# Emitting and pinning one tile's turn behind the last tile's mean and squares

## The chip, the cores and the metric

The kernel runs on one core of one Trainium2 chip. The metric is the device time of one execution in microseconds (us). Engine names are those of the profile: PE is the matmul engine, PEld its weight loads, DVE the vector engine, ACT the scalar engine, POOL the general-purpose engine, SP the engine that issues the transfers here.

## What is computed

Two trunk layers of a diffusion backbone run over 128 context tokens and 512 latent tokens, model width 1024, with shared weights. Each layer has two sublayers, a mixer and a gated convolutional FFN, and each sublayer ends in the same way:

```python
hp = xp * (1 + sc1c) + sh1c                      # modulated input of the mixer
xp = _layernorm(ALPHA * xp + g1c * dp, ln1_g[l], ln1_b[l])
hp = xp * (1 + sc2c) + sh2c                      # modulated input of the FFN
fp = _conv_ffn(hp, ...)
xp = _layernorm(ALPHA * xp + g2c * fp, ln2_g[l], ln2_b[l])
```

The same is done for the latent tokens (`xs`). All arithmetic is in float32; matrix products are made from three products of a high and a low part.

## The kernel before

**Tiles.** The 640 tokens are five tiles of 128 tokens, numbered 0 to 4 (tile 0 is the context). At a sublayer's end `project` goes over the five tiles: for tile i it makes two products of 128x512 (both halves of the width) on PE, `accumulate` multiplies them by a gate and adds them to the residual `ys[i]` on DVE (L498, L502; the L502 instruction also sums the row), and `Norm.stats(i)` makes the layer norm.

**Stats.** `stats(i)` emits, in this order: the negated mean on DVE (L367) and the same over 32 (L368); the sum of squares on ACT (L370, "the squares" below); `affine(i - 1)`, the scale and shift of the tile before with the next sublayer's modulation folded in (L417 multiply, L420 add, for two halves; for tile 3 all four run on DVE and the multiplies are pinned); for tile 4 alone a quicker form on DVE (L377 twice, later L399 twice in `second`); `rstd_of` on POOL (L161, L162); then `between()`; then the normalisation of `ys[i]` in place (L385 on POOL, L389 on ACT). For i of 2 and up `between` is `turn(i - 2)`.

**Turn.** `turn(i)` brings tile i's modulated rows into columns for the next sublayer: for each half of the width four PE transposes into one PSUM tile `B` (L434), then four `split`s, two on each half. A split is a cast on ACT to the high part (L99, reads PSUM) and a subtraction on DVE to the low part (L102, reads the same PSUM tile and the high part). After the loop `project` starts the next sublayer: `next(nxt)` emits its first product over tokens 0 to 257 (24 matmuls of 258 columns, L155 to L157), then `turn(3)`, then a second such product of 24, then `turn(4)`. Tokens 258 to 641, which are tiles 2, 3 and 4, come in a second group of products of 384 columns each, called the second token group below.

**Order.** SP's queue runs as emitted. For the other engines a scheduler orders each queue ahead of the run, by its own estimate of durations and of what is ready, earlier emitted work first. `keep_in_program_order` pins one instruction behind the instruction that was emitted just before it on its engine. Buffers come from pools that are handed on in turn; `ht` and the squares' scratch are of the six `t` buffers.

**Ends.** There are four sublayer ends. At three of them (near 212, 700 and 1043 us) a next sublayer follows; at the last there is no turn.

Of the kernel before, what the change touches and what calls it, by code (L numbers as in the profile page):

```python
# [41 lines left out]
def tile_hybrid_trunk(ctx, tc, xT, x, vecs, tabs, wm0, wm1, wmT, crow, grow, lnrow, bs, w_u, w_v, w_p, w_s, w_pool, w_eo,  # L42
# [4 lines left out]
    dve, act, pe, pool, sp = nc.vector, nc.scalar, nc.tensor, nc.gpsimd, nc.sync  # L47
# [28 lines left out]
    def Tm(shape, dt=F32):  # L76
        return tpool.tile(shape, dt, tag="t", name=nm("t"))

    def M(shape, dt=F32):
        return mpool.tile(shape, dt, tag="m", name=nm("m"))  # L80
# [10 lines left out]
    def B():  # L91
        return psB.tile([128, 512], F32, tag="B", name=nm("B"))

    def f(ap):
        return ap.bitcast(F32)

    def split(hi, lo, src, hi_eng, lo_eng):
        if hi_eng is act:
            act.copy(hi, src)  # L99
        else:  # L100
            hi_eng.tensor_copy(hi, src)
        return lo_eng.tensor_tensor(lo, src, f(hi), ALU.subtract)  # L102


# [16 lines left out]
    def prep(lo_eng=None, pin=False):  # L121
        if not loaded:
            load()
        raw, shape, scale, lo_ = loaded.pop(0)
        lo_eng = lo_eng or lo_
        hi, lo = W(shape, F32R), W(shape, F32R)
        if scale is not None:
            act.activation(hi, raw, AF.Identity, scale=scale)
            dve.scalar_tensor_tensor(lo, raw, scale, f(hi), ALU.mult, ALU.subtract)
            ready.append((hi, lo))  # L130
            return
        with tc.high_priority() if urgent[0] else ExitStack():
            i = split(hi, lo, raw, act, lo_eng or pool)
        if pin:
            tc.keep_in_program_order(i)
        ready.append((hi, lo))
# [22 lines left out]
    def rstd_of(v, e):  # L159
        r = M([128, 1])  # L160
        pool.tensor_tensor(v, v, eps[:, e:e + 1], ALU.add)  # L161
        pool.tensor_tensor(r, v, eps[:, 2:3], ALU.pow)  # L162
        return r
# [168 lines left out]
    def pad_h(h):  # L332
        for t in h[0] + h[1]:
            pool.memset(f(t[:, :, 128:130]), 0.0)
# [16 lines left out]
    class Norm:  # L351
# [11 lines left out]
        def stats(self, i, sums, between=None):  # L363
            y = ys[i]
            a, b = self.rows(i)
            nm, sm, v, nb = (M([128, 1]) for _ in range(4))
            dve.tensor_scalar(nm, sums[0], sums[1], -1.0 / 1024.0, ALU.add, ALU.mult)  # L367
            dve.tensor_scalar(sm, nm, 1.0 / 32.0, None, ALU.mult)  # L368
            jk = Tm([128, D], mybir.dt.bfloat16)
            act.activation(jk, y, AF.Square, bias=sm, scale=1.0 / 32.0, accum_out=v)  # L370
            if i and not self.fast(i - 1):
                self.affine(i - 1)
            if self.fast(i):
                self.ht[i] = [Tm([128, 512]), Tm([128, 512])]
                for h in range(2):
                    sl = slice(h * 512, h * 512 + 512)
                    dve.scalar_tensor_tensor(self.ht[i][h], y[:, sl], nm, a[:, sl], ALU.add, ALU.mult)  # L377
            r = self.rs[i] = rstd_of(v, 0)
            if between is not None:
                between()  # L380
            if i == 4:
                self.second(4)
            if self.nxt is None and self.fast(i):
                return
            pool.tensor_tensor(nb, nm, r, ALU.mult)  # L385
            n = 1 if i == 4 else 2
            for h in range(n):
                sl = slice(h * D // n, (h + 1) * D // n)
                act.activation(y[:, sl], y[:, sl], AF.Identity, bias=nb, scale=r)  # L389
# [35 lines left out]
        def turn(self, i):  # L425
            hi, lo = self.h
            if i == 0:
                pad_h(self.h)
            c = slice(TOK[i], TOK[i] + 128)
            p4 = []  # L430
            for half in range(2):
                ps = B()
                for k in range(4):
                    pe.transpose(ps[:, k * 128:(k + 1) * 128], self.ht[i][half][:, k * 128:(k + 1) * 128], ident)  # L434
                p4.append(ps.rearrange("p (k t) -> p k t", k=4))
            for s in range(4):
                split(hi[s][:, :, c], lo[s][:, :, c], p4[s // 2][:, 2 * (s % 2):2 * (s % 2) + 2, :], act, dve)

        def lazy(self, n=1, out=None):
            w = D // n  # L440
# [93 lines left out]
    def ffn(l, h):  # L534
# [33 lines left out]
        def finish(p, tg, tv):  # L568
            dve.tensor_tensor(tv, tv, tg, ALU.mult)  # L569
            q = max(q for q in range(NQ) if PIECES[q] <= p)  # L570
            gh, gl = pieces[q]
            n = p - PIECES[q]
            if n % 2 == 0:
                gh.append(S([128, 2, T], F32R))
                gl.append(S([128, 2, T], F32R))
            split(gh[n // 2][:, n % 2, :], gl[n // 2][:, n % 2, :], tv, act, dve)
# [99 lines left out]
    def even_first(cb):  # L676
# [90 lines left out]
        with tc.manual_schedule(engines={mybir.EngineType.PE}):  # L767
            warm(16)
            r = mod(0)
            warm(3)  # L770
            turn(0, r)
            for e in (dve, pool, dve):
                prep(e)
            us.extend([take(), take()])
            vu.append(take())
            warm(8)
            r = mod(1)
            for e in range(8):
                product(e, 0)
                if e < 7:  # L780
                    turn(e + 1, r)
                product(e, 1)
                product(e, 2)
                if e < 6:
                    r = mod(e + 2)
                    if e + 5 < 8:
                        load_w(e + 5)
                        load_x(e + 5)
                        if e == 1:
                            load()  # L790
                product(e, 3)
                if e in (0, 2, 4):
                    prep()
                    vu.append(take())
# [762 lines left out]
```

## Time and profile before

| | us |
|---|---|
| median of 3 runs | 1525.19 (1523.65 to 1526.64) |
| profiled execution, its own time | 1525.87 |
| its span, first to last instruction | 1524.1 |
| around the span | 1.8 |

In the rows below, a line of the timeline gives the start in us, the duration in us, the engine, the line of the code, the operation, output<-inputs, shapes, and in brackets how long the engine sat idle before it and what ended that. The mean granted TensorE clock of the whole span is 0.985 of full speed.

### The profile page before, as it was taken

Reading aid. Unit: us, or ns where it says so; the run is one execution under the profiler, and the core shown is the slowest. Engines: PE = TensorE matmul, PEld = TensorE weight load, DVE = VectorE, ACT = ScalarE, POOL = GpSimd, SP = SyncE. Lnnn points to the kernel's source line nnn. Section 1 sums busy time; section 2 is a strip of 40 time slices with the busy share of each in tenths; the row PEclk is TensorE's granted clock in tenths of the full one; section 3 lists DMA queues with packets and bytes.
Section 4 is the critical chain, followed back from the end, with each engine's and each line's share of the span. In section 5 each row is a group of like instructions: output and inputs, shape, how many; then the busy total and the mean of one; then the engine's idle time right before and its main releaser. Section 6 shows DMA issues by size and latency. Waiting matters only on the chain. (4 is left out here: it accounts for less than half of the span.)

```text
span 1524.1 us, 21977 instructions
## 1 busy us (share of the span) xinstructions
PE 1458.7 (96%) x8768; PEld 1316.2 (86%) x8768; DVE 987.7 (65%) x1500; ACT 597.7 (39%) x889; POOL 541.8 (36%) x434
## 2 busy tenths in 40 slices
PE   7989999999999999999997999998999999999997
PEld 5866879989898989888987888787999989898995
DVE  4685688456878697768698477768763334333557
ACT  3422354333132323235775566536333313232223
POOL 2241444333242424543453101864313231232343
PEclk9999999999999999999999999999999999999999
DMA  9544705344454555341321003342433322133231
GB/s 375 219 157 166 277 12 199 107 140 161 157 167 139 164 164 170 99 140 52 112 74 46 1 2 125 122 156 87 162 111 124 99 70 83 34 116 101 71 110 69
DMA packets 54757, 188.10 MB, mean 123 GB/s; under 512 B 6592, under 2 KB 7168, under 8 KB 54656
## 3 DMA queue, kind: packets, MB, share of 16 engines
q1 hardware_dynamic: 54656, 186.71, 36.3%
q8 instruction: 69, 1.13, 0.3%
q14 instruction: 32, 0.26, 0.1%
HBM read 175.96 MB, written 10.72 MB: 122 GB/s over the span
## 5 line engine op out<-in xcount | busy, mean ns | idle before, releaser
L102 POOL TENSOR_TENSOR w<-r,w 128x1024 fp32r<-128x1024 f32 (+2 forms) x133 | 334.6, 2526 | 682.9 <-ACT w L99 667.2
L155 PE MATMUL A<-s,w 128*128 128x258 f32 (+1 forms) x1672 | 524.7, 314 | 19.7 <-ACT t L1227 8.0
L156 PE MATMUL A<-s,w 128*128 128x258 f32 (+1 forms) x1672 | 522.6, 313 | 0.5 <-DVE s L102 0.5
L157 PE MATMUL A<-s,w 128*128 128x258 f32 (+1 forms) x1672 | 521.8, 312 | 0.0
L155 PEld LDWEIGHTS A<-s,w 128*128 128x128 f32 x1672 | 318.0, 190 | 30.8 <-issue 14.7
L156 PEld LDWEIGHTS A<-s,w 128*128 128x128 f32 x1672 | 318.8, 191 | 4.3 <-issue 2.5
L157 PEld LDWEIGHTS A<-s,w 128*128 128x128 f32 x1672 | 318.6, 191 | 2.5 <-issue 2.5
L99 ACT CAST w<-r 128x1024 fp32r<-128x1024 f32 (+2 forms) x181 | 183.8, 1033 | 342.3 <-PE B L156 136.3
L155 PE MATMUL B<-w,s 128*128 128x512 f32 (+2 forms) x734 | 282.9, 387 | 3.5 <-DVE y L495 2.1
L156 PE MATMUL B<-w,s 128*128 128x512 f32 (+2 forms) x734 | 282.4, 385 | 2.3 <-DVE w L102 2.3
L157 PE MATMUL B<-w,s 128*128 128x512 f32 (+2 forms) x734 | 281.4, 384 | 1.0 <-DVE s L102 1.0
L558 DVE SCALAR_TENSOR_TENSOR t<-A,vec,t 128x641 f32<-128x641 f32 x88 | 77.7, 883 | 210.8 <-ACT t L557 210.6
L155 PEld LDWEIGHTS B<-w,s 128*128 128x128 f32 x734 | 138.3, 189 | 32.0 <-DVE y L495 2.3
L156 PEld LDWEIGHTS B<-w,s 128*128 128x128 f32 x734 | 138.4, 189 | 30.1 <-DVE w L102 3.3
L157 PEld LDWEIGHTS B<-w,s 128*128 128x128 f32 x734 | 138.4, 189 | 29.1 <-DVE s L102 1.4
L250 DVE SCALAR_TENSOR_TENSOR t<-r,v 128x1024 bf16<-128x1024 f32 x112 | 160.1, 1440 | 4.7 <-DMA r<-in_wmT_dram 3.7
L99 ACT CAST s<-t 128x642 fp32r<-128x642 f32 x60 | 43.8, 730 | 183.0 <-DVE t L569 147.8
L102 DVE TENSOR_TENSOR w<-r,w 128x1024 fp32r<-128x1024 f32 (+3 forms) x48 | 69.6, 1466 | 61.5 <-ACT w L99 61.4
L495 DVE TENSOR_TENSOR y<-B,y 128x512 f32<-128x512 f32 x80 | 54.7, 687 | 62.3 <-PE B L157 62.2
L557 ACT ACTIVATE t<-A,vec 128x642 f32<-128x642 f32 x88 | 77.6, 882 | 13.9 <-PE A L157 13.8
L559 DVE SCALAR_TENSOR_TENSOR t<-A,vec,t 128x641 f32<-128x641 f32 x88 | 77.8, 885 | 2.5
L561 ACT ACTIVATE t<-t 128x642 f32<-128x642 f32 x44 | 32.6, 742 | 101.6 <-DVE t L559 95.8
(260 smaller groups left out, 1602.7 us busy)
## 6 DMA issues: line engine op xcount, KB each, us to landing
r<-in_w_up_dram SPq DMA_DIRECT2D x88, 512.0 KB, 3.7
r<-in_wmT_dram SPq DMA_DIRECT2D x56, 512.0 KB, 3.3
r<-in_w_dn_dram SPq DMA_DIRECT2D x44, 512.0 KB, 4.2
s<-scr SPq DMA_DIRECT2D x20, 512.0 KB, 7.5
s<-in_wm_dram SPq DMA_DIRECT2D x16, 512.0 KB, 9.3
r<-in_wm_dram SPq DMA_DIRECT2D x16, 512.0 KB, 4.6
kept<-y SPq DMA_DIRECT2D x10, 512.0 KB, 3.5
r<-kept SPq DMA_DIRECT2D x10, 512.0 KB, 3.5
```

The costliest lines, as they stand in the source:

```text
L99: act.copy(hi, src)
L102: return lo_eng.tensor_tensor(lo, src, f(hi), ALU.subtract)
L155: pe.matmul(out, ah, bh, start=i == 0, stop=False)
L156: pe.matmul(out, ah, bl, start=False, stop=False)
L157: pe.matmul(out, al, bh, start=False, stop=i == n - 1)
L250: op = dve.scalar_tensor_tensor(junk, raw, 1.0, cb[s], ALU.mult, ALU.mult, accum_out=mc[l][:, m, s, k:k + 1])
L495: dve.tensor_tensor(acc[i][:, sl], ps, acc[i][:, sl], ALU.add)
L557: act.activation(t, z, AF.Identity, bias=cb, scale=w1)
L558: dve.scalar_tensor_tensor(t[:, 1:], z[:, :T - 1], w0, t[:, 1:], ALU.mult, ALU.add)
L559: dve.scalar_tensor_tensor(t[:, :T - 1], z[:, 1:], w2, t[:, :T - 1], ALU.mult, ALU.add)
L561: act.activation(t, t, AF.Silu)
```

## The change

At tile 4 `between()`, which there is `turn(2)`, is called right after the squares instead of after `rstd_of`. The turn of tile 2 is pinned: each of its ACT casts stands behind the ACT instruction emitted before it (for the first cast that is tile 4's squares), each of its DVE subtractions behind the DVE instruction emitted before it (for the first that is L368 of tile 4), for tile 2 alone. Since `affine(3)` is now emitted after the turn and its L417 was pinned already, L417 of tile 3 now stands behind the turn's last subtraction. No instruction, buffer or transfer is added or removed. At the last sublayer end `between` is None and nothing changes.

```diff
--- before.py
+++ after.py
@@ -94,11 +94,13 @@
     def f(ap):
         return ap.bitcast(F32)
 
-    def split(hi, lo, src, hi_eng, lo_eng):
+    def split(hi, lo, src, hi_eng, lo_eng, pin_hi=False):
         if hi_eng is act:
-            act.copy(hi, src)
+            op = act.copy(hi, src)
         else:
-            hi_eng.tensor_copy(hi, src)
+            op = hi_eng.tensor_copy(hi, src)
+        if pin_hi:
+            tc.keep_in_program_order(op)
         return lo_eng.tensor_tensor(lo, src, f(hi), ALU.subtract)
 
 
@@ -368,6 +370,9 @@
             dve.tensor_scalar(sm, nm, 1.0 / 32.0, None, ALU.mult)
             jk = Tm([128, D], mybir.dt.bfloat16)
             act.activation(jk, y, AF.Square, bias=sm, scale=1.0 / 32.0, accum_out=v)
+            if i == 4 and between is not None:
+                between()
+                between = None
             if i and not self.fast(i - 1):
                 self.affine(i - 1)
             if self.fast(i):
@@ -434,7 +439,9 @@
                     pe.transpose(ps[:, k * 128:(k + 1) * 128], self.ht[i][half][:, k * 128:(k + 1) * 128], ident)
                 p4.append(ps.rearrange("p (k t) -> p k t", k=4))
             for s in range(4):
-                split(hi[s][:, :, c], lo[s][:, :, c], p4[s // 2][:, 2 * (s % 2):2 * (s % 2) + 2, :], act, dve)
+                op = split(hi[s][:, :, c], lo[s][:, :, c], p4[s // 2][:, 2 * (s % 2):2 * (s % 2) + 2, :], act, dve, i == 2)
+                if i == 2:
+                    tc.keep_in_program_order(op)
 
         def lazy(self, n=1, out=None):
             w = D // n
```

## Rows read from the trace of the kernel before

**Rows 1.** The page, part 1: an engine's busy us, share of the span, instructions.

```profile
PE 1458.7 (96%) x8768; PEld 1316.2 (86%) x8768; DVE 987.7 (65%) x1500; ACT 597.7 (39%) x889; POOL 541.8 (36%) x434
```

**Rows 2.** Line L434: what ended PE's idle time before a transpose (us, times).

```profile
  DVE t L420: 15.0, 6
```

**Rows 3.** Timeline of PE at the first of the three ends.

```profile
209.86 0.36 PE L155 MATMUL A<-s,w 128*128 128x258 f32 x1
...
213.44 0.29 PE L157 MATMUL A<-s,w 128*128 128x258 f32 x1
216.12 0.88 PE L434 MATMUL B<-ident,t 128*128 128x128 f32 x4 [2.40 <-DVE t L420]
...
219.17 0.92 PE L434 MATMUL B<-ident,t 128*128 128x128 f32 x4
...
220.77 1.04 PE L434 MATMUL B<-ident,t 128*128 128x128 f32 x8
221.96 0.62 PE L155 MATMUL A<-s,w 128*128 128x384 f32 x2 [0.15 <-ACT s L99]
```

**Rows 4.** Timeline of PE at the second and the third end.

```profile
703.88 0.66 PE L434 MATMUL B<-ident,t 128*128 128x128 f32 x4 [2.40 <-DVE t L420]
...
709.59 0.61 PE L155 MATMUL A<-s,w 128*128 128x384 f32 x2
...
1046.99 0.66 PE L434 MATMUL B<-ident,t 128*128 128x128 f32 x4 [2.38 <-DVE t L420]
...
1051.37 0.62 PE L155 MATMUL A<-s,w 128*128 128x384 f32 x2
```

**Rows 5.** Timeline of ACT at the first end.

```profile
211.44 1.52 ACT L389 ACTIVATE y<-y,m,m 128x512 f32<-128x512 f32 x2 [2.41 <-POOL m L385]
212.87 0.62 ACT L99 CAST s<-B 128x256 fp32r<-128x256 f32 x2
213.71 0.82 ACT L99 CAST s<-B 128x256 fp32r<-128x256 f32 x2 [0.22 <-DVE s L102]
214.43 1.15 ACT L370 ACTIVATE t<-y,m 128x1024 bf16<-128x1024 f32 x1
```

**Rows 6.** Timeline of DVE at the first end.

```profile
211.28 0.08 DVE L502 DVE_READ_ACCUMULATOR y<-t,y 128x1 f32 x1
213.25 0.42 DVE L102 TENSOR_TENSOR s<-B,s 128x256 fp32r<-128x256 f32 x1 [1.89 <-ACT s L99]
213.59 0.20 DVE L367 TENSOR_SCALAR m<-m,m 128x1 f32<-128x1 f32 x1
...
214.45 0.68 DVE L417 TENSOR_TENSOR t<-y,s 128x512 f32<-128x512 f32 x1
...
215.38 0.68 DVE L420 TENSOR_TENSOR t<-t,s 128x512 f32<-128x512 f32 x1
...
216.59 0.75 DVE L377 SCALAR_TENSOR_TENSOR t<-y,m,s 128x512 f32<-128x512 f32 x1
...
218.51 1.41 DVE L399 SCALAR_TENSOR_TENSOR t<-t,m,s 128x512 f32<-128x512 f32 x2
```

**Rows 7.** Timeline of POOL at the first end.

```profile
216.19 0.89 POOL L162 TENSOR_TENSOR m<-m,eps 128x1 f32<-128x1 f32 x1
```

**Rows 8.** Timeline of ACT at the second and the third end.

```profile
699.20 1.52 ACT L389 ACTIVATE y<-y,m,m 128x512 f32<-128x512 f32 x2 [2.40 <-POOL m L385]
...
1042.30 1.52 ACT L389 ACTIVATE y<-y,m,m 128x512 f32<-128x512 f32 x2 [2.40 <-POOL m L385]
```

**Rows 9.** Stretches: PE, PEld, DVE, ACT, POOL busy (instructions), granted clock, DMA share, GB/s.

```profile
95.80:100.20 4.40, 4.39 (x20) 4.40 (x21) 3.60 (x6) 1.46 (x2) 0.00 (x0) 0.50 0.38 119
...
216.40:219.80 3.40, 3.40 (x18) 3.40 (x17) 3.40 (x6) 0.38 (x1) 0.90 (x2) 0.50 0.00 0
817.40:820.50 3.10, 3.08 (x14) 3.08 (x15) 2.88 (x3) 1.66 (x3) 1.63 (x4) 0.50 0.00 0
...
1046.90:1051.30 4.40, 4.28 (x34) 3.87 (x34) 4.40 (x9) 2.13 (x5) 1.18 (x3) 1.00 0.00 0
```

## The prediction

> **What bounds the kernel now.** I read the page first: PE is busy for 96% of the span [rows 1], so what this change can move is PE's idle time, and its clock, at three sublayer ends. Next I asked for the transposes at L434. Their largest wait is for DVE's L420, the end of `affine(3)`: 15.0 us over six waits, 7.2 of them the one long wait that each end shows [rows 2, 3, 4]. Then came the timelines of PE, ACT and DVE at the first end. PE issues 30 matmuls (24 of the next sublayer's first product, six of the second) from 209.86 to 213.44, sits idle for 2.40 us, does tile 3's first transposes at 216.12, and from there to 221.96, where the second token group starts, it works without a gap: 16 transposes and the 18 matmuls that were left [rows 3]. DVE is idle for 1.89 us after tile 4's last sum, because tile 2's first cast waits behind L389 on ACT, and L389 for POOL [rows 5, 6]. From 213.25 to 219.92, the end of the second L399, DVE runs without a break [rows 6]. So the end is a DVE chain that begins with tile 2's casts, and PE's matmuls only partly cover it. The reader should note the order in that chain: L417 of tile 3 runs at 214.45, woven between tile 2's subtractions, and L367 stands behind the first of them.
>
> I measure each end from the start of L389 of tile 3, which the change doesn't touch, to the start of the second token group: 221.96 - 211.44 = 10.52 us, 709.59 - 699.20 = 10.39, and 1051.37 - 1042.30 = 9.07 [rows 3, 4, 5, 8].
>
> **The change part by part.** It adds no instruction and no transfer; SP's queue stands. Everything is order on ACT and DVE, and what the scheduler makes of it on PE.
>
> *Mean and squares go first.* L367 and L368 (0.20 us and less) fall into DVE's idle 1.89 us and cost nothing. The squares start where the first cast stands now, at 212.87 instead of 214.43, 1.56 earlier [rows 5]. What this brings is tile 4's factor: POOL's L162 ends at 217.08 today, but its reader L399 starts at 218.51 [rows 6, 7]. The factor is already 1.43 us early, so the gain is nothing. L389 stays ahead of the squares: it precedes tile 2's casts today, and these were put ahead of the squares, so the scheduler has L389 ready long before.
>
> *The casts go behind the squares.* The first cast moves from 212.87 to 212.87 + 1.15 = 214.02 [rows 5].
>
> *The turn is pinned in its own order.* Two splits share a PSUM tile, and the trace shows a cast on it waiting for the other split's subtraction: the third cast starts at 213.71, 0.22 us idle, as the first subtraction (213.25, 0.42 us) ends [rows 5, 6]. Today casts of the two PSUM tiles alternate, so that hardly hurts. Pinned, the chain is: cast to subtraction 0.38 (212.87 to 213.25), subtraction to next cast 0.46 (213.25 to 213.71), cast to subtraction 0.38, subtraction to subtraction 0.34 (213.25 to 213.59, the next DVE start), subtraction to fourth cast 0.46, cast to subtraction 0.38, last subtraction to L417 0.34: 2.74 us. Today L417 starts 214.45 - 212.87 = 1.58 after the first cast. The value lies between 1.58 (if alternation survived, which the pins exclude) and 2.74; I take 2.74.
>
> *Tile 3 waits for the turn.* L417 is pinned behind the turn's last subtraction: 214.02 + 2.74 = 216.76 instead of 214.45. L420 follows 0.68 later, at 217.44 instead of 215.38, as no subtraction stands between any more: 2.06 us late. Behind L420 come L417 and L420 of the other half, two L377 and two L399. Today that takes 219.92 - 215.38 = 4.54 us [rows 6], so the last L399 ends at 221.98. I keep the L377 inside: they need only tile 4's mean, yet today they run after tile 3's second L417 (216.59) and after subtractions emitted later. I read that as the `t` buffers being handed out as emitted; then they can't slip into the new hole before 214.4.
>
> *PE's order.* The scheduler places tile 3's transposes after the matmuls that it thinks come first. The delay it sees is L367, L368, squares and first cast, 0.20 + 0.14 + 1.15 + 0.38 = 1.87, plus 1.16 for the pinned chain (2.74 - 1.58), less 0.25 (L420 follows L417 in 0.68, not 0.93): 2.8 us. The 18 matmuls left take 18 x (213.44 - 209.86) / 29 = 2.2 us [rows 3]. So I expect all of them ahead of the transposes: PE busy until 215.9, then idle until L420 ends at 218.12, then only transposes with waits between them until the second token group.
>
> *The second token group* starts after tile 4's last transposes: 221.98 + 0.06 (216.06 to 216.12 today) + 0.66 [rows 4, 6] = 222.70, or 11.26 after L389. Against 10.52, 10.39 and 9.07 the three ends lose 0.74 + 0.87 + 2.19 = 3.8 us.
>
> *The clock.* After an idle 2.40 us the first end's matmuls run at a granted clock of 0.50, which is 1.2 of 2.4 GHz, from 216.4 to 219.8; at the third end, after 2.38 us, the clock stays at 1.00, which is why that end is shorter. After other waits the 0.50 lasts 4.40 and 3.10 us [rows 3, 4, 9]. Now PE would be idle or sparsely busy for 6.8 us (215.9 to 222.7), and the half clock would fall on the dense second group. Bounds: nothing (third end) and half of 4.40, 2.2 us an end. Nearest are the low stretches of 3.1 to 3.4, so 1.6 lost; tile 4's transposes before the group take up part; I take 1.2, three times: 3.6 us. The Trainium skill ("TensorE: Matmul & The Clock Gate", Part 1) says that the throttled clock is the default and activity releases it; by that rule alone every one of the three ends would already be low today. The third end, at 1.00 after 2.38 us, disagrees. By the rule the clock term is 3.6 us, by the third end's row it could be 2.4 or less.
>
> **Sum.** 3.8 + 3.6 = 7.4 us. From the profiled execution's 1525.87 (span 1524.1 and 1.8 around it) that gives 1533.3; the profiled run is 0.7 above the median of 1525.19, so I predict 1532.6, some 0.5% slower. About 0.2%, 3 us, is what a measurement can tell from no change.
>
> **The rivals.**
> 1. *The clock holds.* For it: the third end. Against it: 6.8 sparse us instead of 2.4 idle. Time 1525.2 + 3.8 = 1529.0.
> 2. *PE's order stays.* Transposes still follow the sixth matmul and everything behind them shifts by L420's 2.06: 6.2 us, 7.6 if the third end now loses its clock too: 1531.4 to 1532.8. It is inside the forecast's range.
> 3. *The L377 do slip into the hole* while DVE waits for the squares. For it: their data are there at 211.8. Against: they don't run early today. The chain shortens by up to 2 x 0.75 = 1.5 an end: 3.8 - 4.5 = -0.7, with the clock term +2.9: 1524.5 to 1528.1.
> 4. *Faster.* ACT takes the squares before L389 (211.8 to 212.95). First cast 212.95, L417 at 215.69, L420 at 216.37, 0.99 late; with rival 3's 1.5 the last L399 ends at 219.41 and the second group starts at 220.13, 8.69 after L389: 1.83 + 1.70 + 0.38 = 3.9 us less, 1521.3. It decides once DVE's chain ends before today's 219.92. Against it: today's order of L389, casts, squares.
>
> **How the numbers follow.** Forecast with clock loss 0.43, rival 2 0.09, rival 1 0.18, rival 3 0.20, rival 4 0.10. Forecast, 1 and 2 are slower by over 0.2% (0.70); rival 3 is the same but for its upper edge, so slower 0.71, same 0.19, faster 0.10. The range runs from rival 3's lower edge, 1524.5, to the sum with 2.2 an end for the clock, 3.8 + 6.6 = 10.4 or 1535.6, rounded to 1536. The forecast alone spans 1530 to 1536.
>
> **What the changed profile would show.** Squares at 1.4 us after L389 starts, and casts 2.6 after: right start. L417 of tile 3 5.3 after L389's start instead of 3.0, and L377 behind the second L417: the chain is right. 48 matmuls before tile 3's transposes: PE's order is right. Second group 11.3 after L389 with 0.50 beside it: both terms right. L377 before the subtractions, squares before L389, or 1.00 in the second group would make the prediction wrong, in that order of size.

## The result

The changed kernel takes 1532.91 us (median of 6 runs, 1531.46 to 1535.83) against 1525.08 for the kernel before in the same sessions: 1.0054 times, 95% interval 1.0041 to 1.0066. The prediction was 1532.6 and slower. The profiled execution takes 1532.45 us, its span is 1530.6, 6.5 more than before.

In the changed kernel the line numbers have moved: L389 is now L394, L417 is L422, L420 is L425, L377 is L382, L399 is L404, the subtraction L102 is L104, the squares L370 are L372, the transposes L434 are L439, the matmuls L155 to L157 are L157 to L159. The kernels of the experiments have line numbers of their own; the text gives those of before.

What ended PE's idle time before a transpose (us, times), with the weight loads left out, before and in the changed kernel:

```profile
  DVE t L420: 7.2, 3
...
  DVE t L425: 10.7, 6
```

The 15.0 us in six waits of [rows 2] take PE and its weight loads together, which wait at the same moments (7.2 us in three and 7.8 in three). PE's own waits for DVE's L420 before the change are the one long wait of each end and nothing more. Now they are 10.7 us in six: the other half of tile 3 is waited for as well. Timelines of ACT and of DVE at the first end, to be read beside [rows 5, 6]:

```profile
210.99 1.52 ACT L394 ACTIVATE y<-y,m,m 128x512 f32<-128x512 f32 x2 [2.41 <-POOL m L390]
212.41 1.13 ACT L372 ACTIVATE t<-y,m 128x1024 bf16<-128x1024 f32 x1
...
213.54 0.35 ACT L99 CAST s<-B 128x256 fp32r<-128x256 f32 x1
214.39 0.65 ACT L99 CAST s<-B 128x256 fp32r<-128x256 f32 x2 [0.49 <-DVE s L104]
215.58 0.37 ACT L99 CAST s<-B 128x256 fp32r<-128x256 f32 x1 [0.55 <-DVE s L104]
```

```profile
213.93 0.42 DVE L104 TENSOR_TENSOR s<-B,s 128x256 fp32r<-128x256 f32 x1 [2.51 <-ACT s L99]
214.79 0.76 DVE L104 TENSOR_TENSOR s<-B,s 128x256 fp32r<-128x256 f32 x2 [0.44 <-ACT s L99]
215.99 0.42 DVE L104 TENSOR_TENSOR s<-B,s 128x256 fp32r<-128x256 f32 x1 [0.44 <-ACT s L99]
216.33 0.68 DVE L422 TENSOR_TENSOR t<-y,s 128x512 f32<-128x512 f32 x1
217.04 0.69 DVE L425 TENSOR_TENSOR t<-t,s 128x512 f32<-128x512 f32 x1
...
218.25 0.74 DVE L382 SCALAR_TENSOR_TENSOR t<-y,m,s 128x512 f32<-128x512 f32 x1
...
220.18 1.41 DVE L404 SCALAR_TENSOR_TENSOR t<-t,m,s 128x512 f32<-128x512 f32 x2
```

L389 starts at 210.99. The squares follow at 212.41 (1.42 later, forecast 1.4), the first cast at 213.54 (2.55, forecast 2.6), L417 at 216.33 (5.34, forecast 5.3) and L420 at 217.04; the last L399 ends at 221.59 (10.60, forecast 10.54). The chain from first cast to L417 took 2.79 us (forecast 2.74): each of the second and the fourth subtraction is preceded by 0.44 us of idle DVE. POOL and PE at the same end, then PE's second token group at the other two (L389 started at 701.12 and 1046.04 there):

```profile
213.98 0.55 POOL L164 TENSOR_TENSOR m<-m,eps 128x1 f32<-128x1 f32 x1
```

```profile
215.18 0.28 PE L159 MATMUL A<-s,w 128*128 128x258 f32 x1
217.79 0.66 PE L439 MATMUL B<-ident,t 128*128 128x128 f32 x4 [2.33 <-DVE t L425]
219.66 1.11 PE L439 MATMUL B<-ident,t 128*128 128x128 f32 x4 [1.21 <-DVE t L425]
221.07 1.94 PE L439 MATMUL B<-ident,t 128*128 128x128 f32 x8 [0.30 <-DVE t L404]
222.66 0.99 PE L157 MATMUL A<-s,w 128*128 128x384 f32 x2
...
712.80 0.99 PE L157 MATMUL A<-s,w 128*128 128x384 f32 x2
...
1057.72 0.90 PE L157 MATMUL A<-s,w 128*128 128x384 f32 x2
```

POOL's factor is there at 214.53, 5.6 us before L399 reads it, so making the squares earlier bought nothing. All 48 matmuls now stand before tile 3's transposes; PE ends them at 215.46, idles 2.33 us, and then waits twice more, 1.21 and 0.30 us. The second token group starts 11.67 us after L389 at the first end and 11.68 at the others. Stretches of PE at these ends (columns as in [rows 9]):

```profile
215.40:222.60 7.20, 3.36 (x17) 2.69 (x16) 6.38 (x12) 2.54 (x6) 0.00 (x0) 0.73 0.00 0
222.60:225.70 3.10, 3.10 (x12) 3.08 (x12) 2.29 (x7) 2.03 (x6) 0.00 (x0) 0.53 0.00 0
712.70:717.00 4.30, 4.30 (x16) 4.29 (x15) 3.45 (x8) 3.04 (x8) 0.00 (x0) 0.50 0.00 0
1057.60:1061.00 3.40, 3.40 (x20) 3.33 (x19) 2.53 (x7) 2.31 (x7) 0.00 (x0) 0.89 0.03 5
```

PE is busy for 3.36 of the 7.20 us before the group, and then the group itself runs at a granted clock of 0.53, 0.50 and 0.89 of full speed: 1.2 GHz for most of these stretches at the first two ends.

Both kernels issue the same 8768 matmuls, so they can be counted through. From number 1100 to 1200, over the first end, the changed kernel loses 2.30 us; from 3900 to 4000 3.08, from 6000 to 6100 2.80: 8.2 us at the three ends. Elsewhere it has 0.45 us less before the first end, 0.85 less and 0.91 more between the first and the second, and 1.2 less between the second and the third, which leaves the span's 6.5.

### The profile page after: what moved, and what is told of

Read it like the earlier page. It is cut to its first block, busy times and chain, and to the rows that moved or that the text cites. A ratio compares the mean times of both kernels' runs of the same rounds, so it can differ in the third digit from the quotient of the medians.

```text
span 1530.6 us, 21977 instructions
## 1 busy us (share of the span) xinstructions
PE 1462.9 (96%) x8768; PEld 1318.9 (86%) x8768; DVE 986.6 (64%) x1500; ACT 597.8 (39%) x889; POOL 544.4 (36%) x434
## 3 DMA queue, kind: packets, MB, share of 16 engines
q8 instruction: 69, 1.13, 0.3%
## 5 line engine op out<-in xcount | busy, mean ns | idle before, releaser
L104 POOL TENSOR_TENSOR w<-r,w 128x1024 fp32r<-128x1024 f32 (+2 forms) x133 | 338.0, 2552 | 693.0 <-ACT w L99 676.0
L157 PE MATMUL A<-s,w 128*128 128x258 f32 (+1 forms) x1672 | 525.0, 314 | 17.7 <-ACT t L1234 8.0
L159 PE MATMUL A<-s,w 128*128 128x258 f32 (+1 forms) x1672 | 521.4, 312 | 0.0
L157 PEld LDWEIGHTS A<-s,w 128*128 128x128 f32 x1672 | 318.2, 191 | 28.6 <-issue 13.7
L159 PEld LDWEIGHTS A<-s,w 128*128 128x128 f32 x1672 | 318.4, 190 | 2.5 <-issue 2.5
L157 PE MATMUL B<-w,s 128*128 128x512 f32 (+2 forms) x734 | 282.6, 386 | 3.4 <-DVE y L502 2.1
L159 PE MATMUL B<-w,s 128*128 128x512 f32 (+2 forms) x734 | 281.4, 384 | 0.9 <-DVE s L104 0.9
L157 PEld LDWEIGHTS B<-w,s 128*128 128x128 f32 x734 | 138.4, 189 | 31.7 <-DVE y L502 2.3
L159 PEld LDWEIGHTS B<-w,s 128*128 128x128 f32 x734 | 138.5, 189 | 29.1 <-DVE s L104 1.4
L104 DVE TENSOR_TENSOR w<-r,w 128x1024 fp32r<-128x1024 f32 (+3 forms) x48 | 69.6, 1466 | 61.1 <-ACT w L99 60.9
```

The source lines that it names most:

```text
L157: pe.matmul(out, ah, bh, start=i == 0, stop=False)
L159: pe.matmul(out, al, bh, start=False, stop=i == n - 1)
```

## The experiments

All times from L389 of tile 3 below are us after its start, read from the profile of each kernel; the second token group is given for the three ends. "Ratio" is to the kernel before. The diffs are against the changed kernel, unless another is named.

| kernel | L417 | L420 | last L399 ends | second token group | ratio (95%) |
|---|---|---|---|---|---|
| before | 3.0 | 3.9 | 8.5 | 10.5, 10.4, 9.1 | 1 |
| changed | 5.3 | 6.1 | 10.6 | 11.7, 11.7, 11.7 | 1.0054 (1.0041 to 1.0066) |
| 1 emission alone | 3.5 | 4.2 | 8.7 | 10.7, 10.7, 10.6 | 0.9999 (0.9990 to 1.0007) |
| 2 pins alone | 0.85 | 1.6 | 6.5 | 8.1, 8.1, 8.1 | 0.9946 (0.9934 to 0.9959) |
| 3 turn before squares | 4.2 | 4.9 | 9.5 | 10.1, 11.1, 10.7 | 1.0004 (0.9995 to 1.0013) |
| 4 PE's old order | 5.3 | 6.1 | 10.6 | 13.1, 13.3, 12.6 | 1.0066 (1.0054 to 1.0079) |
| 5 PE kept busy | 5.3 | 6.1 | 10.6 | 11.2, 11.2, 11.2 | 1.0030 (1.0020 to 1.0040) |
| 6 splits alternate | 4.5 | 5.2 | 9.7 | 10.8, 10.8, 10.8 | 1.0029 (1.0018 to 1.0040) |
| 7 affine(3) first | 0.85 | 1.6 | 7.1 | 7.7, 7.7, 7.7 | 0.9970 (0.9958 to 0.9981) |
| 8 DVE's pins alone | 0.85 | 1.6 | 6.5 | 8.1, 8.1, 8.1 | 0.9957 (0.9943 to 0.9970) |
| 9 pins alone, alternate | 0.85 | 1.6 | 6.8 | 8.4, 8.4, 8.4 | 0.9972 (0.9961 to 0.9983) |
| 10 L377 early | 6.9 | 7.6 | 5.4 | 12.2, 12.2, 12.1 | 1.0040 (1.0027 to 1.0052) |

### 1. The early emission alone

```diff
-                op = split(hi[s]..., act, dve, i == 2)
-                if i == 2:
-                    tc.keep_in_program_order(op)
+                split(hi[s]..., act, dve)
```

> Theory A (the second token group waits for DVE's chain squares, pinned splits, L417, L420, L377, L399; the pins make that chain 2.06 us longer per end): without the pins the casts run before the squares and alternate again, only L417 still stands behind the turn's last subtraction. L417 of tile 3 about 0.4 us, L420 about 0.2 us later than before the change; the time is that of before, 1525.1, within 1524 to 1527. Rival C (the early emission alone costs, through buffers and priorities): 1532 to 1533, as with the whole change.

Measured: 1525.17 us, 0.9999 times before. DVE's timeline at its first end:

```profile
214.35 0.42 DVE L104 TENSOR_TENSOR s<-B,s 128x256 fp32r<-128x256 f32 x1 [1.88 <-ACT s L99]
214.70 0.20 DVE L369 TENSOR_SCALAR m<-m,m 128x1 f32<-128x1 f32 x1
...
216.01 0.68 DVE L422 TENSOR_TENSOR t<-y,s 128x512 f32<-128x512 f32 x1
216.73 0.69 DVE L425 TENSOR_TENSOR t<-t,s 128x512 f32<-128x512 f32 x1
```

The first subtraction stands before L367 again, and L417 only had to let one more subtraction pass. So the call's new place alone costs nothing that the time shows; the pins do, together with it. Rival C falls. The profiled execution, 1527.77 us, is one of the slower of its twelve: at its third end the granted clock was 0.50 from 1047.5 to 1050.7, behind an idle 2.54 us of PE, where the kernel before kept 1.00 behind 2.38, and the group starts at 10.6 instead of 9.1.

### 2. The pins alone

```diff
-            if i == 4 and between is not None:
-                between()
-                between = None
             if i and not self.fast(i - 1):
                 self.affine(i - 1)
```

> The turn is pinned where it was emitted before, behind affine(3) and the two L377 on DVE and behind the squares on ACT. Theory A: L417 of tile 3 starts as L389's first half ends, about 0.8 us after L389's start instead of 5.3, the last L399 ends about 6.8 us after it instead of 10.6, the second token group starts 8.3 to 9.0 after it instead of 11.7, and PE keeps its full clock: about 4.5 us faster than before the change, 1520.5, within 1518.5 to 1523. Rival D (it is the pinned order of the casts and subtractions themselves, with the squares ahead of the casts, that costs, wherever affine(3) stands): 1528 to 1533.

Measured: 1517.83 us, 0.9946 times before, the fastest kernel of the study, and 0.7 us below the expected range. DVE and PE at its first end (L389 starts at 211.63):

```profile
212.47 0.69 DVE L419 TENSOR_TENSOR t<-y,s 128x512 f32<-128x512 f32 x1 [0.41 <-ACT y L391]
213.20 0.69 DVE L422 TENSOR_TENSOR t<-t,s 128x512 f32<-128x512 f32 x1
...
216.34 0.42 DVE L104 TENSOR_TENSOR s<-B,s 128x256 fp32r<-128x256 f32 x1
216.67 1.40 DVE L401 SCALAR_TENSOR_TENSOR t<-t,m,s 128x512 f32<-128x512 f32 x2
```

```profile
213.95 0.65 PE L436 MATMUL B<-ident,t 128*128 128x128 f32 x4 [0.77 <-DVE t L422]
...
215.81 0.66 PE L436 MATMUL B<-ident,t 128*128 128x128 f32 x4 [0.24 <-DVE t L422]
...
218.64 0.63 PE L436 MATMUL B<-ident,t 128*128 128x128 f32 x4 [0.25 <-DVE s L104]
219.73 0.62 PE L157 MATMUL A<-s,w 128*128 128x384 f32 x2 [0.46 <-ACT s L99]
```

L417 and L420 of tile 3 now use the time in which DVE idled for 1.89 us before [rows 6], tile 2's subtractions come behind them, and PE's waits at this end are 0.77, 0.24, 0.25 and 0.46 us instead of one of 2.40. The pins and the order inside the turn are the same and the squares are just as early, so rival D falls. What decides is whether affine(3) stands before the turn or behind it. Only half of the gain is at the ends. Counted by matmuls from number 1000 to 1200, 3900 to 4000 and 6000 to 6100 they gain 2.0, 1.4 and 0.6 us, 3.9 of the 8.0 by which the span is shorter. This kernel also lacks the wait of 1.4 us for a convolution that the kernel before has at 261.15 (shown further down), and its last FFN is 1.8 us shorter, spread thinly over 2400 matmuls but for 0.5 us at one place; why the latter, no run here shows.

### 3. The turn before the squares

```diff
-            jk = Tm([128, D], mybir.dt.bfloat16)
-            act.activation(jk, y, AF.Square, bias=sm, scale=1.0 / 32.0, accum_out=v)
             if i == 4 and between is not None:
                 between()
                 between = None
+            jk = Tm([128, D], mybir.dt.bfloat16)
+            op = act.activation(jk, y, AF.Square, bias=sm, scale=1.0 / 32.0, accum_out=v)
+            if i == 4 and self.nxt is not None:
+                tc.keep_in_program_order(op)
             if i and not self.fast(i - 1):
                 self.affine(i - 1)
```

> The pinned turn comes before the squares, which are pinned behind it; affine(3) stays behind the turn. Theory A splits the delay of L417 in two halves, 1.15 us for the squares and 1.16 for the pinned order: here only the second is left, L417 about 4.2 us after L389's start, second token group 10.5 to 10.7 after it instead of 11.7; about 3 us less than with the whole change, 1529.5, within 1527.5 to 1531.5. If the squares' place doesn't matter (rival D with the order of casts alone): 1532 to 1533.

Measured: 1525.72 us, 1.0004 times before: a miss by 3.8 us. L417 came as expected (4.2) and the group at 10.1 to 11.1, around the expected 10.5 to 10.7, so the delay does split in the two halves. The time doesn't. Stretches of the second end, before and in the second token group:

```profile
704.00:708.30 4.30, 3.18 (x15) 3.19 (x16) 4.26 (x8) 0.79 (x3) 1.72 (x3) 0.62 0.00 0
...
710.30:714.00 3.70, 3.44 (x19) 3.28 (x20) 2.96 (x7) 2.82 (x8) 0.00 (x0) 1.00 0.00 0
```

Half clock falls on the transposes and ends before the group. So the half of the delay that is left costs 0.6 us of time, which no measurement here can tell from nothing, and the other half 7.2 (1532.91 - 1525.72). Counted by matmuls it is not quite nothing: from number 1100 to 1200 this kernel gains 0.4 us against the one before, from 3900 to 4000 it loses 0.7 and from 6000 to 6100 1.5, so the three ends lose 1.9 us where the whole change loses 8.2, and 1.7 come back elsewhere. Either way the price does not grow evenly with the delay. Two things that the rows show fit this: PE's queue had some slack at the first end, as the last L399 ended 0.85 us before tile 4's transposes started (219.92 to 220.77 by [rows 3, 6]), and the clock is lost in the dense group only with the whole delay. How much each of them carries, this run doesn't part.

### 4. PE's old order

```diff
-            norm.turn(3)
+            def between_matmuls(op):
+                tc.keep_in_program_order(op)
+                seen[0] += 1
+                if seen[0] in (6, 17):
+                    p4.append(norm.columns(3, len(p4), True))
...
             next(nxt)
...
+            norm.turn(3, p4)
             norm.turn(4)
```

`between_matmuls` is called behind each matmul of the second product, and `columns` issues tile 3's four transposes of a half, pinned on PE.

> The whole change, but PE's queue is pinned to the order of before: tile 3's transposes after 30 and after 41 of the 48 matmuls. Theory A: L420's time is unchanged, PE idles 4.5 us before these transposes and the 18 matmuls come after them, so the second token group starts at 12.2 to 12.7 us after L389, but finds the clock partly restored: 1531 to 1534, not better than the whole change by more than 1.5 us. Rival B (the 18 matmuls that moved ahead are the cost): back to 1525 to 1527.

Measured: 1536.00 us, 1.0066 times before, 2 us above the expected range and no better than the whole change. PE at its first end:

```profile
217.06 1.12 PE L436 MATMUL B<-ident,t 128*128 128x128 f32 x4 [4.51 <-DVE t L428]
217.83 2.71 PE L158 MATMUL A<-s,w 128*128 128x258 f32 x11
```

```profile
216.80:221.50 4.70, 4.44 (x21) 4.44 (x22) 4.39 (x8) 0.44 (x2) 0.00 (x0) 0.50 0.00 0
...
223.10:227.00 3.90, 3.88 (x22) 3.50 (x21) 3.17 (x7) 3.02 (x8) 0.00 (x0) 1.00 0.00 0
```

PE idles 4.51 us, and the matmuls that used to fill that time then run at 1.2 GHz until about 221.5. The second token group starts 1.0 to 1.6 us later than in the changed kernel, above the 12.2 to 12.7 that was expected at two of the ends. Moving the 18 matmuls ahead was not the cost, and rival B falls; that it helped is what the group's start says, while the intervals of the two ratios overlap.

### 5. PE kept busy

```diff
             next(nxt)
-            norm.turn(3)
             next(nxt)
+            keep = B()
+
+            def busy(n):
+                for k in range(n):
+                    op = pe.transpose(keep[:, k % 4 * 128:k % 4 * 128 + 128], ident, ident)
+                    tc.keep_in_program_order(op)
+
+            busy(16)
+            norm.turn(3, busy)
             norm.turn(4)
```

The turn calls `busy(8)` between its two halves. These 24 transposes an end go into a tile that nobody reads and are no part of the computation; the second product, which the scheduler puts ahead of the turn anyway, is also emitted ahead of it.

> The whole change, with 24 extra transposes of the identity that nobody reads, 16 pinned before tile 3's first transposes and 8 before the second, in the time in which PE idles. Theory A with the clock term: the second token group starts where it did, 11.7 us after L389, but at a granted clock of 1.00; in the profile of the whole change the half clock covers 2.9, 4.3 and 0.7 us of the three second groups, half of that is 3.9 us: 1529.0, within 1527.5 to 1530.5. Rival E (the clock costs nothing, the group waits for its data anyway): 1532.5 to 1534.

Measured: 1530.19 us, 1.0030 times before. Stretches of its first two ends, before and in the second token group:

```profile
215.00:221.00 6.00, 4.20 (x34) 3.33 (x32) 5.92 (x11) 1.95 (x5) 0.00 (x0) 1.00 0.00 0
221.00:225.00 4.00, 4.00 (x24) 3.69 (x23) 3.48 (x8) 3.13 (x8) 0.00 (x0) 1.00 0.00 0
706.00:712.30 6.30, 4.54 (x37) 3.67 (x36) 5.97 (x11) 2.25 (x5) 0.00 (x0) 1.00 0.00 0
712.30:716.30 4.00, 4.00 (x25) 3.70 (x24) 3.48 (x8) 3.13 (x8) 0.00 (x0) 1.00 0.02 4
```

The clock stays at 1.00 in these stretches, and at the third end too. From 1.0054 to 1.0030 is 0.24%, 3.7 us, or some 1 to 6 by the two intervals: this is what the half clock costs the changed kernel. The mean granted clock says the same of every execution: 0.985 to 0.989 here, 0.979 to 0.985 in the changed kernel. Counted by matmuls, without the extra ones, the three ends lose 0.8, 0.9 and 2.1 us here, 3.8 in all, and 8.2 in the changed kernel, which makes 4.4 for the clock in these two profiles. Of it 0.45 us an end (11.67 to 11.22), 1.4 in all, comes already before the group, as tile 4's eight transposes take 1.29 us instead of 1.94; the group itself has the other 3.0. Rival E falls.

### 6. The splits alternate

```diff
-            for s in range(4):
+            for s in ((0, 2, 1, 3) if i == 2 else range(4)):
```

> The whole change, but the turn's four splits are pinned in the order 0, 2, 1, 3, so that the two PSUM tiles alternate. Theory A: the chain from first cast to L417 shrinks from 2.8 to about 2.0 us, L417 of tile 3 starts 4.6 after L389 instead of 5.3, the second token group 10.9 to 11.0 instead of 11.7: 0.7 us an end, 2.2 in all, 1530.7, within 1529 to 1532. If the order of the splits costs nothing: 1532.5 to 1533.5.

Measured: 1530.15 us, 1.0029 times before. ACT and DVE at its first end:

```profile
214.52 0.62 ACT L99 CAST s<-B 128x256 fp32r<-128x256 f32 x2
```

```profile
214.91 1.62 DVE L104 TENSOR_TENSOR s<-B,s 128x256 fp32r<-128x256 f32 x4 [2.52 <-ACT s L99]
216.44 0.68 DVE L422 TENSOR_TENSOR t<-y,s 128x512 f32<-128x512 f32 x1
```

The four subtractions run without a gap in 1.62 us, L417 starts 0.86 earlier than in the changed kernel, and 0.25% of the 0.54% are gone. The pinned order within the turn is a real part of the cost.

### 7. affine(3) first

```diff
+            if i and not self.fast(i - 1):
+                self.affine(i - 1)
             if i == 4 and between is not None:
                 between()
                 between = None
-            if i and not self.fast(i - 1):
-                self.affine(i - 1)
```

> The whole change with one thing undone: affine(3) is emitted before the early, pinned turn. Theory A (what costs is that tile 3's L417 waits for the turn): L417 0.85 us after L389's start, second token group 8.1 to 8.5 after it, clock 1.00: as fast as with the pins alone, 1518, within 1516.5 to 1520. Rival C (emission before rstd_of costs by itself): 1524 or more.

Measured: 1521.01 us, 0.9970 times before. The two calls swapped, and 0.54% slower turns into 0.30% faster: L417 behind the turn is the cause of the loss. But it is 1 us above the expected range, and slower than the pins alone although its second token group starts earlier, 7.7 instead of 8.1. The following wait of PE at the conv of the first FFN stage, in the kernels before, changed and 7:

```profile
261.15 0.36 PE L155 MATMUL A<-s,w 128*128 128x258 f32 x1 [1.43 <-DVE t L559]
```

```profile
262.15 0.36 PE L157 MATMUL A<-s,w 128*128 128x258 f32 x1 [0.64 <-DVE t L566]
```

```profile
257.03 0.36 PE L157 MATMUL A<-s,w 128*128 128x258 f32 x1 [0.64 <-DVE t L566]
```

The same product waits 1.43 us before, 0.64 in the changed kernel, 0.64 here, and not at all with the pins alone. Counted as in experiment 2 the three ends gain 4.7 us here, against 3.9 with the pins alone, so what this kernel lacks against that one lies outside the ends: its last FFN is as long as before, for one. What the order at the end does to these later parts is not settled here.

### 8. DVE's pins alone

```diff
-                op = split(hi[s]..., act, dve, i == 2)
+                op = split(hi[s]..., act, dve)
```

(in the kernel of experiment 2)

> The pins alone, and of these only those on DVE; the casts on ACT are free, so two of them run before the squares again, 0.5 us. The factor for L399 has more than that to spare. Theory A: time as with all pins, 1517.8, within 1516 to 1519.5; the second token group 8.1 to 8.3 after L389. If squares first was what brought the gain: 1519.5 to 1522.

Measured: 1518.67 us, 0.9957 times before, and its interval holds the ratio of experiment 2. The squares start 1.95 us after L389 instead of 1.43, and nothing that the time shows follows from it.

### 9. The pins alone, alternate

```diff
-            for s in range(4):
+            for s in ((0, 2, 1, 3) if i == 2 else range(4)):
```

(in the kernel of experiment 2)

> The pins alone, with tile 2's four splits in the order 0, 2, 1, 3. Theory A: DVE's chain up to the last L399 gains one subtraction before L399 (0.3 us) and loses the waits between the splits after it; the second token group 7.9 to 8.3 us after L389, as with the pins alone. Time 1517.8, within 1516.5 to 1519.5: nothing more to be had from the order inside the turn.

Measured: 1521.64 us, 0.9972 times before: 2 us above the expected range. The second token group starts at 8.4, 0.3 us later than with the pins alone, as one more subtraction stands before L399. Counted as there, the three ends gain 5.0 us, more than with the pins alone, so the remaining difference lies outside the ends, as in experiment 7: the wait for the convolution is there again with 1.42 us, and the last FFN is as long as before.

### 10. L377 early

```diff
+            if self.fast(i):
+                self.ht[i] = [Tm([128, 512]), Tm([128, 512])]
+                for h in range(2):
+                    sl = slice(h * 512, h * 512 + 512)
+                    dve.scalar_tensor_tensor(self.ht[i][h], y[:, sl], nm, a[:, sl], ALU.add, ALU.mult)
             if i == 4 and between is not None:
                 between()
                 between = None
             if i and not self.fast(i - 1):
                 self.affine(i - 1)
-            if self.fast(i):
-                self.ht[i] = [Tm([128, 512]), Tm([128, 512])]
-                for h in range(2):
-                    sl = slice(h * 512, h * 512 + 512)
-                    dve.scalar_tensor_tensor(self.ht[i][h], y[:, sl], nm, a[:, sl], ALU.add, ALU.mult)
```

> The whole change, with tile 4's two L377 emitted before the early turn. Rival 3 of the prediction said that they stay behind tile 3's L417 only because their buffers are handed out as emitted; then they now run in DVE's hole behind L368, 0.7 to 2.0 us after L389's start. But the scheduler now also puts L399 ahead of the turn's subtractions and tile 4's L389 among its casts, which delays tile 3's L417 to 6.5 to 7.5. Theory A: second token group 10.7 to 11.2 after L389 instead of 11.7, 1.5 to 3 us less than the whole change: 1530.5, within 1529 to 1532.5. If the chain over L417 isn't what counts but tile 4's L399: 1526 or less.

Measured: 1531.86 us, 1.0040 times before. DVE at its first end (L389 starts at 212.69):

```profile
213.04 1.40 DVE L377 SCALAR_TENSOR_TENSOR t<-y,m,s 128x512 f32<-128x512 f32 x2
216.28 0.78 DVE L404 SCALAR_TENSOR_TENSOR t<-t,m,s 128x512 f32<-128x512 f32 x1 [1.83 <-POOL m L164]
...
219.61 0.68 DVE L422 TENSOR_TENSOR t<-y,s 128x512 f32<-128x512 f32 x1
220.33 0.69 DVE L425 TENSOR_TENSOR t<-t,s 128x512 f32<-128x512 f32 x1
...
223.12 0.42 DVE L104 TENSOR_TENSOR s<-B,s 128x256 fp32r<-128x256 f32 x1 [0.44 <-ACT s L99]
```

Emitted early, the L377 do run in DVE's hole, right behind L368. Tile 4's factor form is done at 5.4 us, twice as early as in the changed kernel, and the group still starts at 12.2, a us above the expected range, because tile 3's L417 and L420 come at 6.9 and 7.6, and behind them each subtraction waits 0.42 to 0.44 us for its cast. So the chain over L417 counts, not tile 4's L399.

## Why the prediction was right

*What bounds the end.* The DVE chain from tile 2's casts over L417, L420 and L399 to the second token group. Experiments 1, 2 and 7 show it: with L417 only 0.45 us later than before, no cost that the time shows; with L417 ahead of the turn, a gain. The reading of [rows 2] that led there was half wrong, as it took 15.0 us of waiting for PE's; the argument used only the 7.2 us of the three long waits, which are PE's.

*Mean and squares first bring nothing.* Right: the factor was 5.6 us early, and in experiment 8 another 0.5 us of delay to the squares changes nothing that can be measured.

*Casts behind the squares, pinned order, L417 behind the turn.* Right in size: 1.13 us (213.54 after 212.41) and 2.79 us against 1.15 and 2.74. Experiments 3 and 6 take away one of the two each, and L417 moves by 1.1 and 0.9 us.

*L377 stay inside the chain.* Right (218.25, behind the second L417). Experiment 10 shows that they run early when emitted early; that it is the buffers that hold them, as I read it, was only argued.

*PE's order.* Right: all 48 matmuls are ahead. In experiment 4, with the order of before, the second token group starts 1.0 to 1.6 us later still.

*The second token group.* Mis-sized: 11.67 instead of 11.26 us after L389, so 1.15, 1.29 and 2.61 us at the three ends, 5.05 instead of 3.8. The term that was short is tile 4's transposes, taken at full clock; eight of them took 1.94 us at half clock and 1.29 at full in experiment 5.

*The clock.* Mis-sized the other way, and less even than I took it. I took 3.6 us for the second group alone, 1.2 an end. Counted by matmuls the ends lose 2.30, 3.08 and 2.80 us; without what comes before the group, the group is left with 1.15, 1.79 and 0.19, or 3.1 in all, since at the third end only its first matmuls are slow. The stretches of 4.40 and 3.10 us that I sized this by [rows 9] begin where dense work begins: the granted clock was 0.51 before each of them already, from 93.5 to 95.8 and from 813.7 to 817.4, with PE idle. So it is here: much of the half clock falls on idle time and transposes ahead of the group. Experiment 5 bears the price out in time, within a wide interval: with the transposes taken in, 4.4 us by the counts and 3.7 by the medians. The sentence that weighed the Trainium skill ("TensorE: Matmul & The Clock Gate", Part 1: the throttled clock is the default, activity releases it) asked too much of it. That statement doesn't say that 2.4 us of idle bring the default back, so it doesn't foretell three low ends, and the third end's 1.00 is no evidence against it. In the changed kernel the trace agrees with it: with PE idle for 3.84 of the 7.20 us before the group, and as sparsely at the other two, all three ends fell to 0.50 at some point.

*What the sum left out.* Counted by matmuls the ends lose 8.2 us where the forecast's two terms make 7.4: the first is 1.2 too small, the second 0.5 too large. In this profile 1.7 us (8.2 - 6.5) come back outside the ends, among them the 0.8 us by which the wait for the convolution is shorter. The agreement to 0.3 us of the median is luck: errors of opposite sign cancel in it, and the six executions of the changed kernel alone lie up to 4.4 us apart.

*Rivals.* The clock fell at every end, though at the third only for the group's first matmuls (1). PE's order didn't stay (2), and experiment 4 shows what that would have cost: 1536.0, above the 1532.8 that I gave it. The L377 didn't slip (3). ACT kept L389 ahead of the squares (4).

## What to carry to other kernels

A pin orders not only the pinned instruction but everything that is pinned behind it later: before pinning a group, look for what the next pinned instruction on that engine is and who waits for it. Here the same pins are worth 0.5% with the urgent tile's work emitted ahead of them (half of it at the ends, the rest not fully explained), and cost 0.5% with it emitted behind. An early result was worth nothing here, because its reader stood in a queue that another chain set; and PE's loss at such a place need not be proportional to the delay: here half of the delay cost 1.9 of 8.2 us at the ends and nothing that the time shows. When a profile adds up the waits of a line, see whether PE's matmuls and its weight loads are counted side by side.

## What the runs showed of the hardware

The granted clock is not set by the longest idle stretch alone. One idle stretch of 2.38 us left it at 1.00 and one of 2.40 was followed by 0.50 [rows 3, 4, 9], while 2.33 us followed by transposes with waits of 1.21 and 0.30 us brought 0.50 into the next dense work; 24 unread transposes in the same time kept it at 1.00. And where ACT's casts and DVE's subtractions take turns on one PSUM tile, each released by the other in the trace, four of each took 2.79 us (first cast to L417), against 1.92 (214.52 to 216.44, experiment 6) when two PSUM tiles alternate.
